# Projecting half of the attention's values inside its first six heads

## The chip, the core and the metric

The kernel runs on one core of a Trainium2 chip. Its time is the device time of one execution in microseconds (us). The core has five engines that each work through their own queue in order: PE (TensorE) multiplies, DVE (VectorE), ACT (ScalarE) and POOL (GpSimd) do the element-wise work, and SP (SyncE) issues transfers. A clock throttle grants PE either its full rate, shown as 1.00, or half of it; a stretch with both shows a value between.

## What is computed

A network of two layers on 512 latent and 256 context tokens of width 1024, in float32. Each layer has a feed-forward part, a mixer and a second feed-forward part. The change touches the mixer of the second layer, a differential attention with 8 heads:

```python
def diff_attention_mixer(h_lat, h_ctx, w_in, w_out, lam_vec, sub_w, lam_init, need_ctx):
    ...
        q, k, v = jnp.split(h @ w_in, (DA_QK, 2 * DA_QK), axis=-1)
    ...
    q_l = apply_axial_rope(q_l, cos, sin).astype(h_lat.dtype)
    k_l = apply_axial_rope(k_l, cos, sin).astype(h_lat.dtype)
    ...
    def diff_attend(q, k, v):
        s = jnp.einsum('bhmqd,bhmkd->bhmqk', q, k).astype(jnp.float32)
        p = jax.nn.softmax(s, axis=-1)
        w = p[:, :, 0] - lam * p[:, :, 1]
        return jnp.einsum('bhqk,bhkv->bhqv', w.astype(v.dtype), v)
```

Queries come from the 512 latent tokens, keys and values from all 768. Each head has two maps of 64 dimensions and 128 value columns; its output is normed and then projected by `w_out`.

## The kernel before

Every projection is made in split precision: an operand is written as a high and a low part, and a product takes three matmuls (`mm3`, lines 157 to 159, with weights as the stationary operand; `mm3t`, lines 1326 to 1328, with tokens as the stationary operand). A weight of 512 KB is loaded to a `raw` buffer (4 of them), cast by ACT (high part) and subtracted by DVE or POOL (low part) into a pair of `r4` buffers (8 buffers, so 4 pairs).

`odd_mixer` first projects all values, `proj_v(0)` and `proj_v(1)`: 144 matmuls of 512 columns each, heads 0 to 3 and heads 4 to 7. The settling of the layer ahead (its second half of tokens) is drawn from inside these passes.

Queries and keys come from a generator, `project_heads`. For each head it makes K (24 matmuls of 256 columns for the context, 24 of 512 for the latent tokens, then rope on DVE and a split) and then Q (24 of 512, rope, split), and gives control back ten times a head. The calls of `next` are placed by numbers: 20 pieces (two heads) are made ahead of the first scores, and then 1, 3, 3, 3 pieces in the four query blocks of a head. So head h carries the projections of head h+2, and heads 6 and 7 carry none.

A query block of 128 rows runs like this: `scores` of the block two ahead (12 matmuls into two double banks), maxima on DVE and exponentials on ACT; `mix_maps` (DVE) joins the two maps; `turn` transposes the result on PE and ACT copies it to the tile `late`; the filler pieces follow; then six matmuls with the values into `po` (line 1297). The norm of the head before (`norm_head`, lines 1254 to 1267) is finished behind block 1. Score and turn tiles share three double banks of PSUM, the filler has one bank (`j`), `po` one. A framework schedules the instructions when the kernel is built: it keeps data dependences and moves instructions of a queue past each other, so a queue's order is not quite the order of the program. `Q` and `K` tiles have two buffers.

Places that the text names by lines of before: L1225 scores, L1228 maxima, L1229 exponentials, L1239 joining of maps, L1246 turn, L1248 copy of the turned block, L1297 value matmuls, L1257 to L1266 norm, L1262 its matmul, L1164 to L1167 rope, L1190 and L1203 copies of projected K and Q, L1212 copy of projected values, L117 and L119 high and low part of a split. In the changed file the lines below 1171 stand 48 to 50 further down (L1225 is L1274 there, L1297 is L1345).

Of the kernel before, what the change touches and what calls it, by code (L numbers as in the profile page):

```python
# [13 lines left out]
F32R = mybir.dt.float32r  # L14
BF16 = mybir.dt.bfloat16
AF = mybir.ActivationFunctionType
# [3 lines left out]
P = 128  # L20
D = 1024
KB = D // P
NCTX = 256
NLAT = 512
NT = NCTX + NLAT
# [17 lines left out]
class Net:  # L43
# [589 lines left out]
    def ffn(self, l, p, halves, nxt, ada=((), ()), table=None, first_of_all=False):  # L633
# [7 lines left out]
        with ExitStack() as st:  # L641
# [67 lines left out]
            cols = (slice(full0, full0 + m), slice(full0 + m, full1))  # L709
            quarter = lambda t, K, N: t[:, K * 4:K * 4 + 4, cols[N]]  # L710
            B = lambda K, N: (quarter(self.xh, K, N), quarter(self.xl, K, N))
            made = {}

            def sums_of_inputs():
# [411 lines left out]
    def odd_mixer(self, nxt):  # L1126
        nc, tc, ins = self.nc, self.tc, self.ins
        W = ins["w_in_odd"]
        H = 8
# [1 line left out]
        mm = nc.tensor.matmul  # L1131


        deep, under, before, fill = 2, 12, 20, (1, 3, 3, 3)
        lam_init = 0.8 - 0.6 * math.exp(-0.3)
        with ExitStack() as st:
            pool = st.enter_context(tc.tile_pool(name="att", bufs=1, reuse_waits="tile"))
# [18 lines left out]
            heads = [{} for _ in range(H)]  # L1156
            swap = [(i + 16) % 32 for i in range(32)]
            n_ = self.tmp
            halfs = (slice(0, 64), slice(64, 128))

            def rope(a):

                b, c = n_("shuf"), n_("rot")
                nc.vector.stream_shuffle(out=b, in_=a, mask=swap)  # L1164
                nc.vector.tensor_mul(out=c, in0=b, in1=cs[:, 1, :])
                nc.vector.tensor_mul(out=b, in0=a, in1=cs[:, 0, :])
                nc.vector.tensor_add(out=a, in0=b, in1=c)  # L1167

            filler = lambda: self.ps("j" if "j" in self.psum_bufs else "h")

            def project_heads():

                for h in range(H):
                    w = self.weights(W[8 + h], "gpsimd")
                    K = pool.tile([P, 2, NT], F32R, tag="K", name="K", bufs=2)
                    a = n_("krot")

                    part = lambda src, c0, c1: self.split(K[:, 0, c0:c1], K[:, 1, c0:c1], src)
                    for i, (c0, c1) in enumerate(((0, NCTX), (NCTX, NT))):
                        ps = filler()[:, :c1 - c0]  # L1180
                        for k in range(KB):
                            ks = slice(k * P, (k + 1) * P)
                            self.mm3(ps, w[0][:, ks], w[1][:, ks], self.xh[:, k, c0:c1], self.xl[:, k, c0:c1],
                                     k == 0, k == KB - 1)
                            if k in ((1, 3, 5) if i else (3,)):
                                yield
                        if i == 0:
                            part(ps, 0, NCTX)
                            yield
                    nc.scalar.copy(out=a, in_=ps)  # L1190
                    rope(a)
                    part(a, NCTX, NT)
                    yield
                    w = self.weights(W[h], "gpsimd")
                    ps = filler()
                    for k in range(KB):
                        ks = slice(k * P, (k + 1) * P)
                        self.mm3(ps, w[0][:, ks], w[1][:, ks], self.xh[:, k, NCTX:], self.xl[:, k, NCTX:],
                                 k == 0, k == KB - 1)
                        if k % 2 and k < KB - 1:  # L1200
                            yield
                    a = n_("qrot")
                    nc.scalar.activation(out=a, in_=ps, func=AF.Copy, scale=0.125)  # L1203
                    rope(a)
                    Q = pool.tile([P, 2, NLAT], F32R, tag="Q", name="Q", bufs=2)
                    self.split(Q[:, 0, :], Q[:, 1, :], a)
                    heads[h].update(q=Q, k=K)
                    yield

            def proj_v(g):  # L1210
                wt = [self.weights(ins["w_v_odd"][g, kk]) for kk in range(4)]
                self.token_major(wt, lambda c, t: nc.scalar.copy(out=v[:, c, g * 512:(g + 1) * 512], in_=t))  # L1212

            def scores(h, qb):

                Q, K = heads[h]["q"], heads[h]["k"]
                qs = slice(qb * P, (qb + 1) * P)
# [49 lines left out]
                nc.sync.dma_start(out=mixd[:, h, NCTX:], in_=y)  # L1267

            v = pool.tile([P, NC, D], F32, name="v")
            proj_v(0)  # L1270
            proj_v(1)
            stream = project_heads()
            for _ in range(under):
                next(stream)  # L1274
# [6 lines left out]
            for h in range(H):  # L1281
                po = self.ps("o")
                dg = pool.tile([P, NLAT], F32, tag="dg", name="dg", bufs=2)
                for qb in range(NLAT // P):
                    e, sm = ready.pop(0)
                    i = 4 * h + qb + deep
                    if i < 4 * H:
                        ready.append(scores(i // 4, i % 4))
                    w = mix_maps(e, sm)
# [3 lines left out]
                    t = turn(w, turned[:, qb % 2])  # L1293
# [83 lines left out]
def layout(inputs):  # L1377
    a = {k: np.asarray(v) for k, v in inputs.items()}
    ca = np.ascontiguousarray
    r = {}  # L1380
    x = np.concatenate([a["ctx"][0], a["x"][0]], axis=0).T
    r["x"] = ca(x.reshape(KB, P, NT).transpose(1, 0, 2))
    r["c"] = ca(np.stack([a["c"][0], a["c_ctx"]]))
    r["ct"] = ca(r["c"].reshape(2, KB, P).transpose(2, 1, 0)).reshape(P, 2 * KB)
    w = a["w_ada"][0, :, :2 * D].reshape(KB // 2, 2, P, 2, 4, 256)
    r["w_ada0"] = ca(w.transpose(4, 0, 2, 1, 3, 5)).reshape(4, KB // 2, P, D)
    r["w_ada"] = ca(a["w_ada"].transpose(0, 2, 1).reshape(DEPTH, N_MOD * KB, P, D))
    r["b_ada"] = ca(a["b_ada"].reshape(DEPTH, N_MOD * KB, P).transpose(2, 0, 1))
    ln = np.stack([a["ln_g"], a["ln_b"]], axis=2)
    r["ln"] = ca(ln.reshape(DEPTH, 3, 2, KB, P).transpose(4, 0, 1, 2, 3))  # L1390

    def units(w):
        lead = w.shape[:-2]
        n = w.shape[-1] // P
        w = w.reshape(lead + (KB, P, n, P))
        m = len(lead)
        return ca(w.transpose(tuple(range(m)) + (m + 2, m + 1, m, m + 3))).reshape(lead + (n, P, D))

    def rows(w):
        lead = w.shape[:-2]  # L1400
        nk = w.shape[-2] // (2 * P)
        nq = w.shape[-1] // 512
        w = w.reshape(lead + (nk, 2, P, nq, 512))
        m = len(lead)
        return ca(w.transpose(tuple(range(m)) + (m + 3, m, m + 2, m + 1, m + 4))).reshape(lead + (nq, nk, P, D))

    r["w_ffn_in"] = units(a["w_ffn_in"])
    r["w_ffn_out"] = rows(a["w_ffn_out"])
    r["w_in_even"] = units(a["w_in_even"][0])
    r["w_v_even"] = rows(a["w_in_even"][0][:, 512:1024])  # L1410
    r["w_out_even"] = rows(a["w_out_even"][0])
    r["hg_lb"] = ca(a["hg_lb"][0].reshape(8, P).T)
    r["hg_norm_w"] = ca(a["hg_norm_w"].reshape(1, P).T)
    r["pool_scale"] = ca(a["pool_scale"][0].reshape(4, P).T)
    r["pool_w"] = ca(a["pool_w"][0].transpose(1, 0, 2))
    r["w_in_odd"] = units(a["w_in_odd"][0])
    r["w_v_odd"] = rows(a["w_in_odd"][0][:, 2048:3072])
    r["w_out_odd"] = rows(a["w_out_odd"][0])
    r["da_lambda"] = ca(a["da_lambda"][0])
    r["da_sub_w"] = ca(a["da_sub_w"].reshape(1, P).T)  # L1420
    pos = np.arange(NLAT)
    inv = (10000.0 ** (-np.arange(0, 32, 2, dtype=np.float32) / np.float32(32))).astype(np.float32)
    ang = np.stack([(pos // 64).astype(np.float32)[None, :] * inv[:, None],
                    (pos % 64).astype(np.float32)[None, :] * inv[:, None]])
    cos, sin = np.cos(ang), np.sin(ang)
    cos = np.concatenate([cos, cos], axis=1).reshape(64, NLAT)
    sin = np.concatenate([-sin, sin], axis=1).reshape(64, NLAT)
    r["rope"] = ca(np.stack([np.tile(cos, (2, 1)), np.tile(sin, (2, 1))], axis=1).astype(np.float32))
    s, t = np.arange(P)[:, None] % 32, np.arange(32)[None, :]
    levels = [s == t] + [(s // (2 * m) == t // (2 * m)) & (s // m != t // m) for m in (1, 2, 4, 8, 16)]  # L1430
    r["msk"] = ca(np.stack(levels, axis=1).astype(np.float32))
    edge = np.ones((4, 16), np.float32)
    for g in range(4):
        w = 2 << g
        for i in range(w // 2):
            edge[g, i] = w / (i + w // 2)
# [23 lines left out]
```

## Time and profile before

| | |
|---|---|
| median of 3 runs | 2761.28 us (2757.34 to 2761.32) |
| the profiled execution | 2760.27 us, span 2758.1 us |
| busy share of the span | PE 97%, DVE 71%, ACT 44%, POOL 32% |
| the attention's value passes to its last norm | some 1992 to 2328 us of the span |

The busy time of PE is not its time at peak: matmuls overlap, each is reported longer than the distance to the next one. Where the text gives the price of a matmul it is the distance between starts. A timeline row gives the start, the duration, the engine, the line and the operands; in brackets stands how long the engine was idle before it and what released it. Rows with a count are several equal instructions, with the time from the first one's start to the last one's end.

### The profile page before, as it was taken

How to read it: one execution, taken by the hardware profiler on the slowest of the kernel's cores; microseconds unless marked ns; L12 is line 12 of the kernel's file. 1: busy time of each engine (PE TensorE's matmuls, PEld its weight loads, DVE VectorE, ACT ScalarE, POOL GpSimd, SP SyncE). 2: the span in 40 equal slices, each digit the busy share in tenths (PEclk: the TensorE clock that was granted, in tenths of full speed). 3: DMA queues.
4: the chain of work that ended last, by engine and by line, in shares of the span. 5: the costliest groups of instructions: out<-in, count | busy, mean ns of one | idle time of the engine just before them, and what ended most of it. 6: DMA issues, size and time to landing. Idle time of an engine off the chain costs nothing. (4 is left out here: it accounts for less than half of the span.)

```text
span 2758.1 us, 43943 instructions
## 1 busy us (share of the span) xinstructions
PE 2667.8 (97%) x17386; PEld 2435.0 (88%) x17386; DVE 1966.3 (71%) x2922; ACT 1221.4 (44%) x1922; POOL 888.1 (32%) x680
## 2 busy tenths in 40 slices
PE   8999999999989999999999999999999998999998
PEld 6999988987778789999888999988887777999997
DVE  4899677847764789977786776556827786787666
ACT  3433433634442533433254444423534655555554
POOL 2545300422110554440055444201422211465302
PEclk9999999999999999999999999999999999999999
DMA  6443266521104334426663432265521112433563
GB/s 250 138 155 129 88 244 231 202 78 68 45 22 168 111 131 143 140 91 221 217 201 117 172 123 78 94 230 197 199 77 47 35 39 79 140 100 116 171 212 129
DMA packets 138770, 374.20 MB, mean 136 GB/s; under 512 B 16066, under 2 KB 47170, under 8 KB 138564
## 3 DMA queue, kind: packets, MB, share of 16 engines
q1 hardware_dynamic: 136256, 369.68, 38.6%
q8 instruction: 136, 2.23, 0.3%
q10 hardware_dynamic: 2308, 1.72, 0.2%
q14 instruction: 70, 0.57, 0.1%
HBM read 337.78 MB, written 33.56 MB: 135 GB/s over the span
## 5 line engine op out<-in xcount | busy, mean ns | idle before, releaser
L117 ACT CAST r4h<-raw 128x1024 fp32r<-128x1024 f32 (+1 forms) x322 | 332.8, 1035 | 625.7 <-PE ps L158 325.0
L157 PE MATMUL ps<-xh,r4h 128*128 128x512 f32 (+2 forms) x1732 | 583.7, 339 | 11.4 <-ACT xh L117 7.6
L158 PE MATMUL ps<-xl,r4h 128*128 128x512 f32 (+2 forms) x1732 | 580.8, 336 | 0.5 <-DVE xl L119 0.4
L159 PE MATMUL ps<-xh,r4l 128*128 128x512 f32 (+2 forms) x1732 | 580.4, 336 | 0.4 <-DVE r4l L119 0.4
L119 DVE TENSOR_TENSOR r4l<-raw,r4h 128x1024 fp32r<-128x1024 f32 (+1 forms) x306 | 373.2, 1221 | 223.5 <-ACT r4h L117 163.6
L157 PEld LDWEIGHTS ps<-xh,r4h 128*128 128x128 f32 x1732 | 326.5, 189 | 41.3 <-ACT xh L117 10.1
L158 PEld LDWEIGHTS ps<-xl,r4h 128*128 128x128 f32 x1732 | 327.4, 189 | 22.9 <-DVE xl L119 2.0
L159 PEld LDWEIGHTS ps<-xh,r4l 128*128 128x128 f32 x1732 | 327.8, 189 | 22.2 <-DVE r4l L119 0.9
L157 PE MATMUL ps<-six,r4h 128*128 128x384 f32 (+1 forms) x852 | 278.3, 327 | 6.0 <-ACT c L788 6.0
L157 PE MATMUL ps<-r4h 128*128 128x512 f32 (+1 forms) x768 | 276.4, 360 | 1.1 <-DVE g L903 1.1
L159 PE MATMUL ps<-r4h,r4l 128*128 128x512 f32 (+1 forms) x768 | 275.3, 359 | 0.7 <-DVE r4l L119 0.7
L158 PE MATMUL ps<-six,r4h 128*128 128x384 f32 (+1 forms) x852 | 275.9, 324 | 0.0
L159 PE MATMUL ps<-six,r4l 128*128 128x384 f32 (+1 forms) x852 | 275.4, 323 | 0.0
L158 PE MATMUL ps<-r4l,r4h 128*128 128x512 f32 (+1 forms) x768 | 275.3, 359 | 0.0
L159 PE MATMUL ps<-r4h,spare 128*128 128x256 f32 (+1 forms) x896 | 262.4, 293 | 9.8 <-DVE spare L119 9.8
L157 PE MATMUL ps<-r4h,spare 128*128 128x256 f32 (+1 forms) x896 | 266.0, 297 | 4.0 <-ACT spare L117 4.0
L158 PE MATMUL ps<-r4l,spare 128*128 128x256 f32 (+1 forms) x896 | 261.4, 292 | 0.0
L760 POOL TENSOR_TENSOR raw<-raw,late 128x512 f32<-128x512 f32 x71 | 93.6, 1319 | 400.4 <-DVE r4l L119 388.5
L119 DVE TENSOR_TENSOR r4l<-late,r4h 128x1024 fp32r<-128x1024 f32 x71 | 106.1, 1495 | 115.1 <-PE ps L158 97.2
L159 PEld LDWEIGHTS ps<-r4h,spare 128*128 128x128 f32 x896 | 174.8, 195 | 13.2 <-DVE spare L119 11.3
L157 PEld LDWEIGHTS ps<-r4h,spare 128*128 128x128 f32 x896 | 175.0, 195 | 8.6 <-ACT spare L117 4.6
L185 DVE SCALAR_TENSOR_TENSOR trash<-spare 128x1024 bf16<-128x1024 f32 x112 | 181.1, 1618 | 1.0 <-DMA spare<-in_w_ada 0.9
(313 smaller groups left out, 5646.6 us busy)
## 6 DMA issues: line engine op xcount, KB each, us to landing
raw<-in_w_ffn_in SPq DMA_DIRECT2D x176, 512.0 KB, 3.5
raw<-in_w_ffn_out SPq DMA_DIRECT2D x176, 512.0 KB, 4.3
spare<-in_w_ada SPq DMA_DIRECT2D x80, 512.0 KB, 5.3
six<-in_w_ada SPq DMA_DIRECT2D x64, 512.0 KB, 5.7
g<-late_g SPq DMA_DIRECT2D x88, 128.0 KB, 2.1
six<-g SPq DMA_DIRECT2D x44, 256.0 KB, 3.7
raw<-in_w_in_even SPq DMA_DIRECT2D x20, 512.0 KB, 3.5
raw<-in_w_in_odd SPq DMA_DIRECT2D x16, 512.0 KB, 3.4
```

The source lines that it names most:

```text
L117: self.copied = self.nc.scalar.copy(out=h, in_=src)
L119: eng.tensor_sub(out=l, in0=src, in1=h.bitcast(F32))
L157: mm(out=ps, lhsT=h, rhs=xh, start=first, stop=False)
L158: mm(out=ps, lhsT=h, rhs=xl, start=False, stop=False)
L159: mm(out=ps, lhsT=l, rhs=xh, start=False, stop=last)
L185: nc.vector.scalar_tensor_tensor(out=self.tmp("trash").bitcast(BF16), in0=r, scalar=1.0, in1=self.c_bc[v], op0=ALU.mult, op1=ALU.mult, acc ...
L760: nc.gpsimd.tensor_sub(out=a12, in0=a12, in1=sums[:, 512:])
```

## The change

The second value pass is taken out of the stretch ahead of the attention. The values of heads 4 to 7 are projected in six pieces inside heads 0 to 5: a piece makes two chunks of 128 tokens for two heads (256 columns), 48 matmuls of 256 columns into one filler bank. Their weights come in another layout, two loads of 512 KB for each two heads; one pair of parts lies in a buffer of its own (`wv`), the other in an `r4` pair that stays taken for three heads, and POOL makes both low parts. The generator is rearranged: ahead of the scores stand K0, Q0 and K1 (16 pieces instead of 20); head h then carries Q of head h+1, a value piece (h < 6) and K of head h+2, in 4, 4, 3 and 3 pieces. Q7 comes in head 6.

```diff
-        deep, under, before, fill = 2, 12, 20, (1, 3, 3, 3)
+        deep, under, before, fill = 2, 12, 16, (4, 4, 3, 3)
...
+            def late_weights(g):
+
+                r = []
+                for i in range(2):
+                    raw = self.raw()
+                    nc.sync.dma_start(out=raw, in_=ins["w_v_late"][g, i])
+                    if i:
+                        r.append(self.pair(raw, 1024, "gpsimd"))
+                    else:
+                        r.append([pool.tile([P, 1024], F32R, tag="wv", name="wv", bufs=2) for _ in range(2)])
+                        self.split(*r[-1], raw, "gpsimd")
+                return r
+
+            def project_values(i):
+
+                g, chunks = i // 3, (i % 3 * 2, i % 3 * 2 + 1)
+                if i == 0:
+                    later.append(late_weights(0))
+                ps = filler()
+                for k in range(KB):
+                    wh, wl = later[g][k // 4]
+                    ws = slice(k % 4 * 256, (k % 4 + 1) * 256)
+                    for x, c in enumerate(chunks):
+                        s = slice(c * P, (c + 1) * P)
+                        self.mm3t(ps[:, x * 256:(x + 1) * 256], wh[:, ws], wl[:, ws], self.xh[:, k, s],
+                                  self.xl[:, k, s], k + x == 0, k + x == KB)
+                    if k % 2 and k < KB - 1:
+                        yield
+                nc.scalar.copy(out=v[:, chunks[0]:chunks[1] + 1, 512 + g * 256:512 + (g + 1) * 256],
+                               in_=ps.rearrange("p (c f) -> p c f", c=2))
+                if i == 2:
+                    later.append(late_weights(1))
+                yield
+
+            def project_heads():
+
+                yield from project_keys(0)
+                yield from project_queries(0)
+                yield from project_keys(1)
+                for h in range(1, H):
+                    yield from project_queries(h)
+                    if h < 7:
+                        yield from project_values(h - 1)
+                    if h + 1 < H:
+                        yield from project_keys(h + 1)
...
-            proj_v(0)
-            proj_v(1)
+            proj_v()
...
-    r["w_v_odd"] = rows(a["w_in_odd"][0][:, 2048:3072])
+    r["w_v_odd"] = rows(a["w_in_odd"][0][:, 2048:2560])
+    w = a["w_in_odd"][0][:, 2560:].reshape(2, 4, P, 2, 256)
+    r["w_v_late"] = ca(w.transpose(3, 0, 2, 1, 4)).reshape(2, 2, P, D)
```

`project_keys` and `project_queries` hold the two halves of the old loop body unchanged.

Where the instructions of a head then stand is read from the orders of the queues. On PE, in a steady head, around the end of K's context part (the matmuls of 256 columns) and the start of its latent part (512 columns), before:

```order
L159 MATMUL ps<-xh,r4l 128x256
L1297 MATMUL ps<-late,v 128x128 x6
L1262 MATMUL pss<-sq,ones_v 128x512
L157 MATMUL ps<-xh,r4h 128x512
L158 MATMUL ps<-xl,r4h 128x512
L159 MATMUL ps<-xh,r4l 128x512
```

and in the changed kernel, where L1345 are the value matmuls, L1274 the scores and L1295 the turn:

```order
L159 MATMUL ps<-xh,r4l 128x256
L1345 MATMUL ps<-late,v 128x128 x5
L157 MATMUL ps<-xh,r4h 128x512
L158 MATMUL ps<-xl,r4h 128x512
L159 MATMUL ps<-xh,r4l 128x512
L157 MATMUL ps<-xh,r4h 128x512
L158 MATMUL ps<-xl,r4h 128x512
L159 MATMUL ps<-xh,r4l 128x512
L1345 MATMUL ps<-late,v 128x128
L1274 MATMUL pss<-K,Q 128x384 x12
L1295 MATMUL pss<-ident,e 128x128 x6
```

Between the two parts of K stood six value matmuls and the norm; now five value matmuls stand there, and the sixth and the next scores come behind two k-steps of the latent part.

On DVE, which reads K's context part out of the filler bank (`K<-ps,K`), in a steady head before, with the norm's steps L357 to L1266:

```order
L119 TENSOR_TENSOR K<-ps,K 128x256
L1239 SCALAR_TENSOR_TENSOR e<-e,sm 128x768
L357 SCALAR_TENSOR_TENSOR t<-sq,t 128x512
L358 TENSOR_SCALAR t<-t 128x512
L359 TENSOR_TENSOR y<-y,t 128x512
L1266 SCALAR_TENSOR_TENSOR y<-o,da_sub_w,y 128x512
L1228 TENSOR_REDUCE sm<-pss 128x1 x2
```

and now, with L1277 the maxima, L1284 to L1288 the joining of the maps and L1315 the norm's last step:

```order
L1277 TENSOR_REDUCE sm<-pss 128x1
L357 SCALAR_TENSOR_TENSOR t<-sq,t 128x512
L1277 TENSOR_REDUCE sm<-pss 128x1
L358 TENSOR_SCALAR t<-t 128x512
L359 TENSOR_TENSOR y<-y,t 128x512
L1284 RECIPROCAL sm<-sm 128x1
L1315 SCALAR_TENSOR_TENSOR y<-o,da_sub_w,y 128x512
L119 TENSOR_TENSOR K<-ps,K 128x256
L1285 SCALAR_TENSOR_TENSOR sm<-sm,nlam 128x1
L1288 SCALAR_TENSOR_TENSOR e<-e,sm 128x768
```

The reading of the context part stood ahead of the norm's steps and now stands behind them.

On ACT, after the last projection, Q7 (its copy is `qrot<-ps`, the high part of its split `Q<-qrot`, the copy of a turned block `late<-pss`), before:

```order
L1203 ACTIVATE qrot<-ps 128x512
L1257 COPY o<-ps 128x512
L1258 ACTIVATE sq<-o 128x512
L117 CAST Q<-qrot 128x512
L1248 COPY late<-pss 128x768
L1229 ACTIVATE e,sm<-pss,sm 128x768 x2
```

and now:

```order
L1204 ACTIVATE qrot<-ps 128x512
L117 CAST Q<-qrot 128x512
L1297 COPY late<-pss 128x768
L1278 ACTIVATE e,sm<-pss,sm 128x768 x2
L1313 COPY sq<-pss 128x512
```

The two steps of the norm between them have gone ahead; the split of Q7 stands ahead of the turned copy in both.

## Rows read from the trace of the kernel before

**Rows 1.** Windows: busy us (and counts) of each engine, granted clock, DMA share, GB/s.

```profile
core 0: us, PE busy (x) PEld busy (x) DVE busy (x) ACT busy (x) POOL busy (x), PEclk, DMA share, GB/s
...
2100.00:2105.00 5.00, 5.00 (x30) 4.26 (x30) 2.00 (x4) 0.80 (x1) 0.00 (x0) 0.66 0.00 0
...
2160.00:2191.50 31.50, 29.80 (x197) 24.38 (x195) 25.39 (x38) 18.73 (x34) 8.46 (x8) 1.00 0.10 34
...
2290.00:2295.00 5.00, 5.00 (x26) 4.34 (x26) 2.08 (x5) 0.99 (x2) 0.45 (x1) 0.50 0.00 0
```

**Rows 2.** Timeline of ACT: the copy of the same value chunk in both passes.

```profile
2025.34 0.59 ACT L1212 COPY v<-ps 128x512 f32<-128x512 f32 x1 [1.29 <-PE ps L1328]
...
2059.07 0.59 ACT L1212 COPY v<-ps 128x512 f32<-128x512 f32 x1 [1.29 <-PE ps L1328]
```

**Rows 3.** Timeline of PE: first matmul of K0's context part and of its latent part.

```profile
2059.58 0.28 PE L157 MATMUL ps<-xh,r4h 128*128 128x256 f32 x1
...
2062.46 0.39 PE L157 MATMUL ps<-xh,r4h 128*128 128x512 f32 x1
```

**Rows 4.** Timeline: first scores, split of K1, first turn, first turn of head 1.

```profile
2082.23 1.14 PE L1225 MATMUL pss<-K,Q 64*128 64x384 f32 x9
...
2087.70 0.62 ACT L117 CAST K<-krot 128x512 fp32r<-128x512 f32 x1 [4.02 <-DVE krot L1167]
...
2099.91 0.85 PE L1246 MATMUL pss<-ident,e 128*128 128x128 f32 x6 [2.09 <-DVE e L1239]
...
2128.34 0.87 PE L1246 MATMUL pss<-ident,e 128*128 128x128 f32 x6
```

**Rows 5.** Timeline of PE: head 3, from its first turn to head 4's.

```profile
2191.46 0.88 PE L1246 MATMUL pss<-ident,e 128*128 128x128 f32 x6
...
2196.46 1.32 PE L1225 MATMUL pss<-K,Q 64*128 64x384 f32 x11 [0.99 <-ACT e L1229]
...
2200.07 1.50 PE L1297 MATMUL ps<-late,v 128*128 128x128 f32 x12
2201.40 1.02 PE L1262 MATMUL pss<-sq,ones_v 128*128 128x512 f32 x2
2203.00 0.51 PE L157 MATMUL ps<-xh,r4h 128*128 128x512 f32 x1 [0.57 <-DVE K L119]
...
2215.41 0.87 PE L1246 MATMUL pss<-ident,e 128*128 128x128 f32 x6
...
2223.00 0.87 PE L1246 MATMUL pss<-ident,e 128*128 128x128 f32 x6
```

**Rows 6.** Timeline of ACT and DVE behind the norm matmul of head 3.

```profile
2202.47 0.58 ACT L1264 COPY sq<-pss 128x512 f32<-128x512 f32 x1
2202.53 0.42 DVE L119 TENSOR_TENSOR K<-ps,K 128x256 fp32r<-128x256 f32 x1
...
2205.07 0.69 DVE L357 SCALAR_TENSOR_TENSOR t<-sq,t 128x512 f32<-128x512 f32 x1 [1.21 <-ACT t L356]
...
2206.99 0.75 DVE L1266 SCALAR_TENSOR_TENSOR y<-o,da_sub_w,y 128x512 f32<-128x512 f32 x1
...
2207.66 1.81 DVE L1228 TENSOR_REDUCE sm<-pss 128x1 f32<-128x768 f32 x2
```

**Rows 7.** Timeline from the end of Q7's matmuls to the last norm.

```profile
2282.59 1.50 PE L1297 MATMUL ps<-late,v 128*128 128x128 f32 x12
...
2287.76 0.62 ACT L117 CAST Q<-qrot 128x512 fp32r<-128x512 f32 x1 [2.39 <-DVE qrot L1167]
...
2289.13 2.93 PE L1297 MATMUL ps<-late,v 128*128 128x128 f32 x12 [3.00 <-ACT late L1248]
...
2305.11 0.87 PE L1246 MATMUL pss<-ident,e 128*128 128x128 f32 x6
...
2309.66 0.87 PE L1246 MATMUL pss<-ident,e 128*128 128x128 f32 x6
...
2326.14 2.07 PE L1262 MATMUL pss<-sq,ones_v 128*128 128x512 f32 x2 [2.73 <-POOL sq L1259]
```

More of the change, by code (lines that the diff above doesn't have):

```diff
@@ L1169, in odd_mixer @@
             filler = lambda: self.ps("j" if "j" in self.psum_bufs else "h")
[L1171 to L1195, printed above, removed]
@@ L1196, in project_heads, with project_keys @@
+            def project_keys(h):
+                w = self.weights(W[8 + h], "gpsimd")
+                K = pool.tile([P, 2, NT], F32R, tag="K", name="K", bufs=2)
+                a = n_("krot")
+                part = lambda src, c0, c1: self.split(K[:, 0, c0:c1], K[:, 1, c0:c1], src)
+                for i, (c0, c1) in enumerate(((0, NCTX), (NCTX, NT))):
+                    ps = filler()[:, :c1 - c0]
                     for k in range(KB):
                         ks = slice(k * P, (k + 1) * P)
-                        self.mm3(ps, w[0][:, ks], w[1][:, ks], self.xh[:, k, NCTX:], self.xl[:, k, NCTX:],
+                        self.mm3(ps, w[0][:, ks], w[1][:, ks], self.xh[:, k, c0:c1], self.xl[:, k, c0:c1],
@@ L1199, in project_heads @@
                                  k == 0, k == KB - 1)
-                        if k % 2 and k < KB - 1:
+                        if k in ((1, 3, 5) if i else (3,)):
                             yield
[L1202 to L1212, printed above, removed]
+                    if i == 0:
+                        part(ps, 0, NCTX)
+                        yield
+                nc.scalar.copy(out=a, in_=ps)
+                rope(a)
+                part(a, NCTX, NT)
+                heads[h].update(k=K)
+                yield
@@ new lines, in project_queries @@
+            def project_queries(h):
+                w = self.weights(W[h], "gpsimd")
+                ps = filler()
+                for k in range(KB):
+                    ks = slice(k * P, (k + 1) * P)
+                    self.mm3(ps, w[0][:, ks], w[1][:, ks], self.xh[:, k, NCTX:], self.xl[:, k, NCTX:],
+                             k == 0, k == KB - 1)
+                    if k % 2 and k < KB - 1:
+                        yield
+                a = n_("qrot")
+                nc.scalar.activation(out=a, in_=ps, func=AF.Copy, scale=0.125)
+                rope(a)
+                Q = pool.tile([P, 2, NLAT], F32R, tag="Q", name="Q", bufs=2)
+                self.split(Q[:, 0, :], Q[:, 1, :], a)
+                heads[h].update(q=Q)
+                yield
@@ new lines, in project_values @@
+            def project_values(i):
+                g, chunks = i // 3, (i % 3 * 2, i % 3 * 2 + 1)
+                if i == 0:
+                    later.append(late_weights(0))
+                ps = filler()
+                for k in range(KB):
+                    wh, wl = later[g][k // 4]
[4 more added lines that the diff above has]
+                                  self.xl[:, k, s], k + x == 0, k + x == KB)
+                    if k % 2 and k < KB - 1:
+                        yield
+                nc.scalar.copy(out=v[:, chunks[0]:chunks[1] + 1, 512 + g * 256:512 + (g + 1) * 256],
+                               in_=ps.rearrange("p (c f) -> p c f", c=2))
+                if i == 2:
+                    later.append(late_weights(1))
+                yield
@@ new lines, in project_heads, with proj_v @@
+            def project_heads():
[8 more added lines that the diff above has]
+                        yield from project_keys(h + 1)
+            later = []
+            def proj_v():
+                wt = [self.weights(ins["w_v_odd"][0, kk]) for kk in range(4)]
+                self.token_major(wt, lambda c, t: nc.scalar.copy(out=v[:, c, :512], in_=t))
```

## The prediction

> **What bounds the kernel now.** I read the page first: PE is busy for nearly all of the span and its clock row is full, so a change pays only where PE idles, waits inside a busy stretch, or runs at half clock. Then the windows of the attention [rows 1]: in head 2 PE is busy 29.80 of 31.50 us, DVE 25.39 and ACT 18.73, so PE is the bound with small holes; and there are two places where the granted clock falls, 0.66 after the attention's first wait and 0.50 after the wait in head 6. Last I read the timeline of PE through the start, one steady head and the last two heads, and looked up what ended each hole. In what follows (h,q) is query block q of head h. "Turn" is the six transposes of a block (L1246), "mix" its six value matmuls (L1297), "scores" its twelve (L1225).
>
> Before the attention starts, PE runs without a hole, so work taken out there comes off the time whole. Inside the heads, work put in costs what PE does, less the holes it fills. The change moves work from the first place to the second; the gain is holes filled, and no arithmetic goes away.
>
> **Unit prices.** The second half of the values is one pass of 144 matmuls of 512 columns. The same copy comes 2025.34 and 2059.07 in the two passes [rows 2]: 33.7 us, or 0.234 a matmul. A matmul of 256 columns costs 0.120: the 24 of K's context part start at 2059.58 and the next piece at 2062.46 [rows 3]. So Q of a head costs 24 x 0.234 = 5.62, K 24 x 0.120 + 5.62 = 8.50, and a value piece 48 x 0.120 = 5.76. The six pieces are 34.6 against 33.7, 0.8 us more work.
>
> **Part 1, the values leave the stretch ahead of the attention: -33.7 us.** K0's first matmul follows the first value pass instead of the second. Its weights are then due 33.7 us earlier; they take the buffers that the second pass's weights had, which showed no wait, so I add nothing.
>
> **Part 2, the start.** From the first scores to the first turn of head 1 it takes 2128.34 - 2082.23 = 46.1 us [rows 4]. Its work before: seven score blocks, four turns, four mixes, Q1, K2, Q2. After: V0 in place of Q2. One block of scores, turn and mix without filler costs 3.37: between the turns at 2215.41 and 2223.00 lie 7.59 us with 18 matmuls of 512 in them [rows 5]. Four blocks 13.5, three more score blocks of 1.25 each 3.75, fillers 5.62 + 5.76 + 8.50 = 19.9: 37.1 us, about the same as before, where 9 us were lost. What is lost after: the first turn needs a chain on DVE of six score maxima (0.9 each, as the pair in [rows 6]), the rope of K1 between them (4.0, as ACT's wait for it in [rows 4]), the low half of K1 (0.7) and the first mix of maps (1.7), 12 to 13 us from the first scores, while PE has 36 score matmuls and 23 of Q1, 9.1 us. So 3.7 are lost there, and I add 1.7 for a slow stretch like 2100 to 2105 (5 us at 0.66) [rows 1]. That gives 42.5, **-3.6 us**. Bounds: no slow stretch and a shorter chain, 41; nothing gained, 46.1.
>
> **Part 3, the steady heads.** The period is 2223.00 - 2191.46 = 31.5 us [rows 5]. Its work is four blocks of 3.37, a norm of 1.0, Q and K 14.1: 28.6. The other 2.9 are holes: scores wait 0.99 for an exponential, because the block ahead has only a 1.5 us piece in front of it; the filler after the norm waits 0.57 until K's context part has been read out of the one filler bank [rows 5]; the rest is pieces split around the wait. After, the pieces are even: Q, then V, then half of K twice. The first hole needs scores to follow too closely on the scores ahead of them; with 4.2 us of filler at least in every block they come 6 us or more later, and it closes. The second stays and moves. The order of PE shows K's 256-column matmuls, then five of the six mix matmuls, then K's next piece, so the cover is 5/6 of a mix, 1.2 us, where it was a mix and a norm. The order of DVE shows the reading of the context part behind the whole norm. By rows [rows 6]: from the copy of the norm at 2202.47 to DVE's first step on it 2.6; a maximum 0.9; its last three steps until 2207.74, 2.0 after that first one; the reading itself 0.42; with gaps some 7.1 us after the norm. PE is there after scores, turn, K's context part and 5/6 of a mix, at 6.0. So a wait of 1.1 us a head. From below: 0.5, the 0.57 of the rows as it is now. From above: 1.7, if the reading takes as long from the end of K's context part as now (2203.00 - 2200.07 = 2.9) with 1.2 of cover. I take 1.1, the sum of the rows in their new order, which lies between them. A head is then 13.5 + 1.0 + 19.9 + 1.1 = 35.5 us.
>
> From the first turn of head 1 to the end of Q7's matmuls it is 2282.59 - 2128.34 = 154.25 us before [rows 4, 7]. After, five heads of 35.5, then the turn (0.63) and Q7 (5.62 and a step) that now stand in head 6: 183.8. **+29.5 us.** DVE's 25.4 us spread over 35.5 instead of 31.5, and ACT takes on 0.6 for a piece and 0.7 for weights a head. Neither comes near the period. The weights' low halves go to POOL, which is busy 8.5 us a head, and the four new loads of 512 KB stand in the SP queue two uses ahead.
>
> **Part 4, the tail.** From Q7's end to the last norm: 2326.14 - 2282.59 = 43.55 us [rows 7]. Here Q7's rope was on DVE, and ACT waited 2.39 for it in the cast that stands ahead of the copy of the turned weights; PE waited 3.00 for that copy and then ran at 0.50. After, the same two instructions stand in the same order behind Q7, one block later: I expect the stall and the slow stretch to stay and only move to (6,1). What goes is one bare block, since Q7 now fills (6,0): 2309.66 - 2305.11 = 4.55 [rows 7]. 39.0, **-4.5 us**. If the stall falls short of the clock's drop the tail gains 2.5 more; if norm and stall add up in one block it loses 2.
>
> **Sum.** -33.7 - 3.6 + 29.5 - 4.5 = -12.3 us. The profiled execution took 2760.27 us (span 2758.1 and 2.2 around it), 1.0 under the median of the runs. 2760.3 - 12.3 = **2748.0 us**.
>
> **The clock, weighed.** The granted clock was 0.66 in the stretch after a wait of 2.09 us [rows 1, 4] and 0.50, its lower level of 1.2 GHz, after one of 3.00 [rows 1, 7]. In a head built like the one with waits of 0.99 and 0.57 [rows 5] it was 1.00. The Trainium skill (TensorE: Matmul & The Clock Gate, "A second HAM failure mode: psum-queue depth-cycling") says that small idle times between matmul groups which cycle through PSUM can make the clock go back and forth between its levels. By that rule the new wait on the one filler bank would cost clock in every head, the second rival below; the steady heads of this trace do not agree so far.
>
> **Rivals.** (1) The holes stay and only change place: PE meets in each head as much waiting as now (2.9 instead of 1.1), for example because DVE's order, with the norm ahead of the reading, runs later than its rows sum to. 5 x 1.8 = 9.0 back: 2757.0; with the start's 3.6 also back 2760.6. For it: the stated cover is smaller than before, and every wait here is set by in-order queues of ACT and DVE. Against: the 0.99 has a cause that the even pieces remove. (2) Slower: the wait on the filler bank reaches 2.0 us and halves the clock behind it, six times. Each costs 1.0 us more wait and 1.7 (5 us at 0.66) to 2.5 (5 us at 0.50) of slow matmuls: 6 x 2.7 to 6 x 3.5, 16 to 21 us, 2764 to 2769. It decides from a wait of 2.0 us, twice my estimate; against it stands that the longest wait of head 3 is 0.99 [rows 5] and that head 2, built alike, ran at 1.00 [rows 1]. (3) That the pieces don't come where they are said to be is ruled out by the order of PE: the 48 value matmuls stand in block 1 of heads 0 to 5, Q of the next head in block 0.
>
> **How the numbers follow.** My forecast 0.79, rival 1 0.15, rival 2 0.06. The bounds: heads 0.5 to 1.7 of wait, -3 to +3; start -1.5 to +3.6; tail -2.5 to +2. All the low ends together give 2741.0, all the high ends 2756.6; rival 1 at 2757.0 takes the upper end to 2758. Range 2741 to 2758. A measurement of this kernel tells some 0.2%, 5.5 us, from no change. Faster by more than that (under 2755.8), the forecast: 0.79; within, rival 1: 0.15; slower, rival 2: 0.06.
>
> **What would show it.** In the profile after: the first scores some 33.7 us earlier; no wait of scores for exponentials in heads 1 to 5; one wait a head of PE for DVE's K, about 1.1 us; a period between first turns of 35.5 us; a wait of 2.5 to 3 us for the turned copy in (6,1) with the clock at half behind it; and the last norm starting 12 us earlier than at 2326.14. I am wrong if the period is above 37 us, or if the granted clock is under 1.00 within heads 1 to 5, and in the first step if K0 waits for its weights.

## The result, and the profile after

The changed kernel takes 2744.09 us (median, 2742.66 to 2746.52) beside 2759.31 of the kernel before: a ratio of 0.9946, 95% interval 0.9929 to 0.9964. Two later sets of runs gave 2739.56 beside 2759.32 and 2741.75 beside 2760.11. By these medians the change takes off 15 to 20 us; 12.3 were forecast.

The profiled execution has a span of 2742.4 us. I cut the attention of every trace at the same five events: the first copy of values on ACT, the first scores, the first turn of head 1, the first turn of head 6, the last norm. The first and the last of these are 310.20 us apart before and 291.36 after. Ahead of the first copy both kernels run the same instructions, and yet the three profiles of the changed kernel reach it at 2018.99, 2018.18 and 2015.64 (before at 2015.94). That is scatter between executions, so in what follows I compare the stretch from the first copy to the last norm and not spans.

Timeline of ACT, PE and DVE of the changed kernel: first value copy, the scores of head 0 and the wait between them, DVE's first joining of maps, first turn of head 0, the scores of a later block, first turn of head 1 (these answer to [rows 2, 4]):

```profile
2018.99 2.02 ACT L1261 COPY v<-ps 128x512 f32<-128x512 f32 x4
...
2051.55 2.35 PE L1274 MATMUL pss<-K,Q 64*128 64x384 f32 x18
...
2055.69 1.33 PE L1274 MATMUL pss<-K,Q 64*128 64x384 f32 x6 [0.43 <-ACT e L1278]
...
2057.61 1.34 PE L1274 MATMUL pss<-K,Q 64*128 64x384 f32 x6
...
2059.53 1.31 PE L1274 MATMUL pss<-K,Q 64*128 64x384 f32 x6
...
2062.21 1.94 DVE L1288 SCALAR_TENSOR_TENSOR e<-e,sm 128x768 f32<-128x768 f32 x2
...
2064.14 0.82 PE L1295 MATMUL pss<-ident,e 128*128 128x128 f32 x6
...
2076.24 1.34 PE L1274 MATMUL pss<-K,Q 64*128 64x384 f32 x12
...
2093.23 0.87 PE L1295 MATMUL pss<-ident,e 128*128 128x128 f32 x6
```

One value pass stands ahead of the scores now: 2051.55 - 2018.99 = 32.56 us, where it was 66.29. The wait of 2.09 before the first turn [rows 4] is gone.

Timeline of PE of the changed kernel, head 3 (answers to [rows 5]; the trace holds two records for each value matmul, so a mix of six is x12):

```profile
2163.43 0.88 PE L1295 MATMUL pss<-ident,e 128*128 128x128 f32 x6
...
2180.14 1.02 PE L1311 MATMUL pss<-sq,ones_v 128*128 128x512 f32 x2
...
2185.95 1.28 PE L1345 MATMUL ps<-late,v 128*128 128x128 f32 x10
...
2187.74 0.51 PE L157 MATMUL ps<-xh,r4h 128*128 128x512 f32 x1 [0.51 <-DVE K L119]
...
2198.40 0.87 PE L1295 MATMUL pss<-ident,e 128*128 128x128 f32 x6
```

The period is 2198.40 - 2163.43 = 34.97 us. The wait of scores for an exponential (0.99) is gone; one wait is left, for DVE's reading of K's context part.

Timeline of PE and, between its rows, of ACT, from the end of Q7's matmuls to the last norm (answers to [rows 7]):

```profile
2274.65 1.50 PE L1345 MATMUL ps<-late,v 128*128 128x128 f32 x12
...
2279.36 0.62 ACT L117 CAST Q<-qrot 128x512 fp32r<-128x512 f32 x1 [3.63 <-DVE qrot L1167]
2279.89 0.79 ACT L1297 COPY late<-pss 128x768 f32<-128x768 f32 x1
...
2280.73 1.60 PE L1345 MATMUL ps<-late,v 128*128 128x128 f32 x12 [2.53 <-ACT late L1297]
...
2291.09 1.60 PE L1345 MATMUL ps<-late,v 128*128 128x128 f32 x12 [0.89 <-ACT late L1297]
...
2310.35 2.07 PE L1311 MATMUL pss<-sq,ones_v 128*128 128x512 f32 x2 [2.74 <-POOL sq L1308]
```

The stall for the turned copy stands where it was forecast, in (6,1). ACT's queue still holds the cast of Q7 ahead of that copy. The 0.89 is what a block of the tail without filler waits for the copy anyway.

Windows (columns as in [rows 1]), first head 3 and the stretch around the stall in the changed kernel, then the same five us around the same stall in its third profile:

```profile
2163.43:2198.40 34.97, 34.46 (x245) 29.95 (x243) 25.32 (x38) 19.30 (x35) 8.34 (x8) 1.00 0.09 31
...
2280.00:2285.00 5.00, 4.27 (x32) 3.27 (x32) 3.52 (x7) 4.27 (x8) 0.45 (x1) 1.00 0.01 2
```

```profile
2277.00:2282.00 5.00, 4.59 (x20) 3.26 (x22) 2.75 (x5) 2.67 (x6) 0.45 (x1) 0.66 0.00 0
```

In the heads the granted clock is 1.00. Behind the stall of 2.53 us it stayed at 1.00 in one execution and was 0.66 in the others.

### The profile page after: what moved, and what is told of

Its sections match the earlier page's. It is cut to its first block, busy times and chain, and to the rows that moved or that the text cites. A ratio compares the mean times of both kernels' runs of the same rounds, so it can differ in the third digit from the quotient of the medians.

```text
span 2742.4 us, 44233 instructions
## 1 busy us (share of the span) xinstructions
PE 2660.8 (97%) x17530; PEld 2437.4 (89%) x17530; DVE 1962.8 (72%) x2918; ACT 1220.4 (45%) x1922; POOL 900.3 (33%) x684
```

## The experiments

Every ratio is against runs of the kernel before on the same chip in the same set. This table has the four stretches of every profile (us). Clock is the granted clock of five us from the stall of head 6 on ((6,0) before and in e2_values, (6,1) in the others):

| | values | start | heads 1 to 5 | end | sum | clock | ratio, 95% |
|---|---|---|---|---|---|---|---|
| before | 66.29 | 46.11 | 156.92 | 40.88 | 310.20 | 0.50 | 1 |
| changed | 32.56 | 41.68 | 175.10 | 42.02 | 291.36 | 1.00 | 0.9946 [0.9929, 0.9964] |
| after_again | 32.56 | 41.74 | 175.11 | 43.68 | 293.09 | 0.66 | 0.9931 [0.9919, 0.9943] |
| changed_third | 32.56 | 41.71 | 175.10 | 43.69 | 293.06 | 0.66 | 0.9933 [0.9921, 0.9945] |
| e1_queries | 66.29 | 36.46 | 155.49 | 43.68 | 301.92 | 0.66 | 0.9971 [0.9961, 0.9981] |
| e2_values | 32.56 | 47.29 | 177.10 | 41.20 | 298.15 | 0.50 | 0.9954 [0.9942, 0.9967] |
| e3_uneven | 32.55 | 43.74 | 192.04 | 43.68 | 312.01 | 0.66 | 1.0007 [0.9997, 1.0018] |
| e4_q7_dve | 32.54 | 41.74 | 175.10 | 41.16 | 290.54 | 1.00 | 0.9925 [0.9914, 0.9937] |
| e5_norm2 | 32.56 | 41.74 | 171.04 | 44.22 | 289.56 | 0.66 | 0.9929 [0.9917, 0.9941] |
| e6_start | 30.72 | 45.10 | 175.08 | 42.03 | 292.93 | 1.00 | 0.9941 [0.9929, 0.9952] |
| e7_all | 30.72 | 45.09 | 171.05 | 42.16 | 289.02 | 1.00 | 0.9922 [0.9910, 0.9934] |
| e8_two | 32.56 | 41.72 | 171.05 | 42.15 | 287.48 | 1.00 | 0.9904 [0.9888, 0.9919] |

The stretches of the changed kernel repeat within 0.1 us over its three profiles, except the end, which has two values 1.7 us apart, one for each clock. So a single profile can tell apart edits that the times of some runs can't. The kernel before and each edit have one profile; the slow clock in it is that of one execution.

**The changed kernel again (after_again, changed_third).**

> The changed kernel once more, so that the others are compared on the same chip. Both theories: 12 to 19 us under the kernel before; period of a steady head 35.0 us, a wait of 0.5 us a head for K's context part.

> The changed kernel once more, unaltered, so that the version below stands beside it in the same hour: a ratio of 0.993 to 0.995 against the kernel before.

Measured: 2739.56 and 2741.75 us, 19.8 and 18.4 us under the kernel before in the same set. The start, the heads and the value pass repeat to 0.1 us.

**One part alone: the queries (e1_queries) or the values (e2_values).**

```diff
--- e1_queries: values as before, queries half a head later
+        deep, under, before, fill = 2, 12, 16, (4, 0, 3, 3)
...
-                    if h < 7:
-                        yield from project_values(h - 1)
...
+            proj_v(0)
+            proj_v(1)
--- e2_values: values in the heads, queries a head ahead as before
+        deep, under, before, fill = 2, 12, 20, (5, 3, 3, 3)
...
+                for h in range(H):
+                    if h > 1:
+                        yield from project_values(h - 2)
+                    yield from project_keys(h)
...
```

> Values as before, only the queries half a head later: Q1 is projected inside head 0, Q7 in head 6, blocks carry 4, 0, 3, 3 pieces. Theory H (the gain is holes of PE that are filled, from either half of the change): no work is removed, yet 10 to 14 us under the kernel before: about -9 at the start (46.1 to about 37 us from the first scores to head 1's first turn), +3 to +5 in heads 1 to 5 with Q7, -4.5 to -8 in the tail. Rival V (the value pieces alone bring the gain, the query shift only makes room): within 2 us of the kernel before.

> Queries as before (a head ahead), only the values of heads 4 to 7 go into blocks 0 of heads 0 to 5 ahead of K's first half. Theory H: 8 to 16 us under the kernel before: first scores 33.7 us earlier, the 0.99 us wait of scores for exponentials gone from heads 1 to 5, so a steady head of about 35.2 us, and the stall of about 3 us with a slow clock still in head 6. Rival Q (the query shift alone brings the gain, moving values costs its 0.8 us): 0 to 2 us over the kernel before. If both halves fill the same holes, the two single gains add up to clearly more than the whole.

Measured: 2751.15 us and 2746.27 us, 8.2 and 13.1 under the kernel before. The values lie in their range; the queries miss theirs of 10 to 14. Their start came as expected (-9.65), but from head 1's first turn on they take 1.4 us more, where between 5.0 less and 0.5 more was expected. In the stretch the queries alone take off 8.3 us, the values 12.1, together 20.3, and the whole change 17.1 to 18.8. To see where they overlap, subtract from each stretch the matmul time that the edit only moves into or out of it (Q 5.62; a value piece 5.76, one in the start and five in heads 1 to 5). What is left is time that PE saved:

| | start | heads 1 to 5 | end |
|---|---|---|---|
| e1_queries | -9.65 + 5.62 = -4.0 | -1.4 | 2.80 - 5.62 = -2.8 |
| e2_values | 1.18 - 5.76 = -4.6 | 20.18 - 28.8 = -8.6 | +0.3 |
| changed | -4.43 - 5.76 + 5.62 = -4.6 | 18.18 - 28.8 = -10.6 | 1.14 - 5.62 = -4.5 |

Not all of it is holes. Windows of the kernel before behind its stall and over its heads 1 to 5, and of heads 1 to 5 of the changed kernel:

```profile
2288.00:2296.00 8.00, 6.49 (x30) 5.55 (x30) 5.08 (x8) 3.31 (x7) 0.45 (x1) 0.57 0.00 1
...
2128.34:2285.26 156.92, 148.73 (x972) 121.96 (x970) 126.97 (x190) 92.83 (x166) 32.90 (x32) 1.00 0.10 36
```

```profile
2093.23:2268.33 175.10, 172.25 (x1212) 149.74 (x1211) 128.97 (x188) 98.23 (x174) 43.97 (x36) 1.00 0.13 45
```

Slow clock took 3.4 us of the end before (8 us at 0.57) and 1.7 of its start (5 us at 0.66 [rows 1]). In the end, e2_values has the same 3.4, e1_queries 1.7 and the changed profile none; without it the end's row is -1.1, +0.3 and -1.1, so the end belongs to the queries. In the heads PE's idle time fell from 8.2 to 2.9 us, which is half of the 10.6; the other half is no idle time in these windows, and where it lies was not shown.

The heads add up (1.4 + 8.6 = 10.0 of 10.6). The start's saving is the same one for both parts: with either of them the wait of 2.09 us and the slow clock behind it are gone. That counts some 4.0 us twice. Less the 0.6 in the heads and 0.3 in the end by which the whole is better than the sum, it makes the 3.2 us by which the single gains exceed the whole in the two profiles with e1_queries' clock (1.5 in the one whose clock stayed up).

Timeline of PE, the queries alone, one head's waits:

```profile
2163.49 0.44 PE L1272 MATMUL pss<-K,Q 64*128 64x384 f32 x1 [0.67 <-ACT Q L117]
2164.45 1.31 PE L1272 MATMUL pss<-K,Q 64*128 64x384 f32 x11 [0.52 <-ACT e L1276]
...
2170.82 0.50 PE L157 MATMUL ps<-xh,r4h 128*128 128x512 f32 x1 [0.30 <-DVE K L119]
```

Without a value piece in block 1, the holes stay in the heads and change place (0.67 + 0.52 + 0.30). So it is the filler in every block that closes them, as the prediction said of the 0.99. The values alone, with filler in every block, show no wait above 0.25 us in four of heads 1 to 5, and 0.74 in head 2.

**The pieces made uneven again (e3_uneven).**

```diff
-        deep, under, before, fill = 2, 12, 16, (4, 4, 3, 3)
+        deep, under, before, fill = 2, 12, 16, (0, 8, 3, 3)
...
-                    for _ in range(fill[qb]):
+                    for _ in range((4, 4, 3, 3)[qb] if h == 6 else fill[qb]):
```

> The changed kernel with the same pieces, but none in block 0 and eight (Q and the value piece) in block 1 of heads 0 to 5; head 6 as in the changed kernel. Theory H: the wait of scores for exponentials comes back because two blocks of scores follow each other with about 1 us of filler between: 1.0 to 2.0 us a head, a period of 36 to 37 us, 6 to 12 us over the changed kernel. Rival (the hole hung on the order of Q and K, not on how much filler a block has): within 2 us of the changed kernel.

Measured: 2759.71 us; the whole gain is gone, although the same work stands in the same heads (only Q and the value piece share a block, and block 0 has next to none). Timeline of PE, head 1 and then head 2 of this kernel, and the windows of head 1, of the place behind the second wait, and of head 3:

```profile
2096.20 1.31 PE L1274 MATMUL pss<-K,Q 64*128 64x384 f32 x11 [1.30 <-ACT e L1278]
...
2158.96 0.51 PE L157 MATMUL ps<-xh,r4h 128*128 128x512 f32 x1 [2.28 <-DVE K L119]
```

```profile
2091.15:2129.53 38.38, 36.93 (x245) 31.40 (x243) 25.42 (x38) 19.41 (x35) 8.31 (x8) 0.96 0.10 35
...
2158.00:2163.00 5.00, 4.04 (x16) 2.94 (x16) 0.90 (x2) 0.00 (x0) 0.00 (x0) 0.66 0.01 3
...
2170.72:2207.44 36.72, 35.32 (x245) 30.05 (x243) 25.36 (x38) 19.46 (x35) 8.25 (x8) 1.00 0.09 30
```

Each of heads 1 to 5 has a wait of 1.24 to 1.30 us of scores for an exponential, as expected. Head 3, with the clock up, has a period of 36.72 instead of 34.97. Behind two of these waits, in heads 1 and 4, the granted clock fell (0.96 over head 1, 0.66 in the five us from 2097); behind the other three it did not. In head 2 it fell behind another wait, 2.28 us for DVE's reading of K's context part: that is the second rival of the prediction as it was put, a wait on the filler bank of more than 2.0 us. Heads 1 and 4 take 38.3 us and more, head 2 41.2. The loss of 20 us against the changed kernel is more than the 6 to 12 expected; the three slow stretches are some 5 of it (1.7 each).

**The stall in (6,1) (e4_q7_dve).**

```diff
-                self.split(Q[:, 0, :], Q[:, 1, :], a)
+                if h == H - 1:
+                    nc.vector.tensor_copy(out=Q[:, 0, :], in_=a)
+                    nc.vector.tensor_sub(out=Q[:, 1, :], in0=a, in1=Q[:, 0, :].bitcast(F32))
+                else:
+                    self.split(Q[:, 0, :], Q[:, 1, :], a)
```

> The changed kernel with one edit: the high part of the last head's queries is cast by DVE, and not by ACT. Theory (ACT does its queue in order, and the turned copy that the mix of block (6,1) wants stands behind the cast of the queries, which waits for PE's last query matmul): the wait of 2.53 us ahead of the mix in head 6 shrinks to under 1 us, the granted clock stays at 1.00 there, and the time lies 1.5 to 2.5 us below the changed kernel's, up to 4 us where the clock had fallen behind the wait; against the kernel before a ratio near 0.9925. Rival (the copy is late for another reason, as DVE's reading of the queries' sum): the wait stays within 0.5 us of 2.53 and the time is the changed kernel's, a ratio of 0.993 to 0.9945.

Measured: 2739.31 us. Timeline of this kernel, ACT's turned copy and PE's waits in head 6:

```profile
2275.59 0.80 ACT L1301 COPY late<-pss 128x768 f32<-128x768 f32 x1 [2.50 <-PE pss L1299]
```

```profile
2276.44 1.60 PE L1349 MATMUL ps<-late,v 128*128 128x128 f32 x12 [0.89 <-ACT late L1301]
...
2279.82 1.33 PE L1278 MATMUL pss<-K,Q 64*128 64x384 f32 x11 [0.56 <-ACT e L1282]
...
2282.98 1.27 PE L1349 MATMUL ps<-late,v 128*128 128x128 f32 x9 [1.02 <-ACT late L1301]
```

ACT now waits for PE's turn and not for Q7, and PE's stall falls from 2.53 to the 0.89 of a block without filler. So the cause was ACT's in-order queue. The gain was smaller than the 1.5 to 4 us expected: the stretch is 0.8 us shorter than in the changed profile whose clock stayed up, 2.5 shorter than in the two whose clock fell, since of the 1.64 us 0.56 came back in the next scores. The time alone doesn't separate it from the changed kernel.

**The wait in each head (e5_norm2).**

```diff
-                    if qb == 1:
+                    if qb == 2:
```

> The changed kernel with one edit: the norm of a head is finished behind block 2 of the next head, and not behind block 1, so that DVE comes to the context part of the keys before the steps of the norm. Theory (the wait of 0.52 us in each head is DVE's, which has the norm's steps ahead of the keys in its queue): that wait goes in the five heads that show it, the heads' period falls from 34.97 to about 34.45 us, the work of PE alone, and the time by 2.5 to 3 us. Rival (DVE's total work or another reader of the same bank sets the period): the wait moves to another row of the head, the period stays at 34.9 to 35.0, and the time is the changed kernel's within 0.5 us.

Measured: 2739.53 us. Timeline of PE and DVE of this kernel in head 4, where DVE reads K, then windows of its head 5 and of the stretch behind the stall, and a window of head 3 of e2_values:

```profile
2215.69 1.50 PE L1345 MATMUL ps<-late,v 128*128 128x128 f32 x12
...
2217.07 0.42 DVE L119 TENSOR_TENSOR K<-ps,K 128x256 fp32r<-128x256 f32 x1
...
2217.55 0.74 PE L157 MATMUL ps<-xh,r4h 128*128 128x512 f32 x1
```

```profile
2228.26:2262.47 34.21, 34.21 (x244) 29.88 (x243) 26.37 (x40) 19.95 (x36) 4.29 (x6) 1.00 0.14 47
...
2275.00:2280.00 5.00, 5.00 (x30) 4.13 (x30) 3.00 (x5) 1.70 (x4) 0.45 (x1) 0.66 0.00 0
```

```profile
2166.72:2201.82 35.10, 35.01 (x245) 29.97 (x243) 25.77 (x38) 19.24 (x35) 8.80 (x8) 1.00 0.09 31
```

The wait is gone and PE is busy for the whole period, which falls by 0.76 us to 34.21. That is 0.25 more than the 0.51 in brackets. Whether a wait costs more than its own length is not shown: the edit also moves the norm's matmuls, and a head of e2_values is busy for 35.01 of 35.10 us, so the same work takes 0.8 us more or less in another order, without a wait in either. Over heads 1 to 5 the edit gains 4.1 us. Some comes back in the end: with the clock up it is 42.15 in e8_two, with this edit, and 41.16 in e4_q7_dve, without it. In this execution the clock fell behind the unchanged stall of 2.53, and the end took 44.22; the stretch is 3.5 us shorter than in the two profiles of the changed kernel whose clock fell too. The time alone does not separate the two kernels.

**The start (e6_start), and all three edits (e7_all).**

```diff
-        deep, under, before, fill = 2, 12, 16, (4, 4, 3, 3)
+        deep, under, before, fill = 2, 10, 14, (4, 4, 3, 3)
...
-                yield from project_keys(1)
                 for h in range(1, H):
                     yield from project_queries(h)
+                    if h == 1:
+                        yield from project_keys(1)
...
-                    for _ in range(fill[qb]):
+                    for _ in range(6 if h + qb == 0 else fill[qb]):
```

> The changed kernel with the start in another order: keys 0, queries 0 and queries 1 ahead of the first head's turned maps, and keys 1 as the filler of its blocks, where the changed kernel has keys 1 ahead and queries 1 as filler. Theory (in the start PE is short of work that needs no map: keys are 8.5 us of matmuls and queries 5.6, so the longer one covers more of the first maps' chain on ACT and DVE): from the first scores to head 1's first turn 38 to 40 us instead of 41.7, the later heads unchanged at 35.0, the time 2 to 3.5 us below the changed kernel's. Rival (the chain of the first maps is covered already, and keys 1 come late for the scores of head 1): a new wait of 1 us or more ahead of head 1's scores, and the time is the changed kernel's or up to 2 us above it.

> The three edits together: the last queries cast by DVE, the norm behind block 2, keys 1 as the filler of head 0. If the three waits are separate holes of PE on one chain, their gains add up: 6 to 8 us below the changed kernel, a ratio of 0.990 to 0.991 against the kernel before. If they share a cause (DVE's queue, which gets more work in head 6 by the first edit and later norms by the second), less than 4 us below it, a ratio of 0.992 or more, with a wait of PE for DVE in head 6 or 7 that the changed kernel does not show.

Measured: 2743.92 us and 2738.93 us. Timeline of PE, start of e6_start:

```profile
2048.34 2.73 PE L1275 MATMUL pss<-K,Q 64*128 64x384 f32 x18 [0.97 <-ACT Q L117]
...
2059.63 0.50 PE L157 MATMUL ps<-xh,r4h 128*128 128x512 f32 x1 [0.92 <-DVE K L119]
```

My theory of the start fell. The scores come 1.84 us earlier (keys 1 out, queries 1 in, less the new wait of 0.97 for the split of Q0), but the start is 3.4 longer: 1.6 us lost. Work that needs no map was not what was lacking: PE's waits in the changed kernel's start are 0.43 and 0.28 us. With keys 1 as filler PE meets two waits for ACT's and DVE's splits that queries 1 in that place avoid. With all three edits the ratio is 0.9922, where 0.990 to 0.991 was expected of separate waits. By this number a shared cause would be right, but its sign, a wait for DVE in head 6 or 7, is not there; the stretch of 289.02 has the norm's 4.1 us gained and 1.6 lost in the start.

**The two edits that gained (e8_two):** those of e4_q7_dve and e5_norm2.

> The changed kernel with the two edits whose traces showed a gain, and the start as it is: the last queries cast by DVE and the norm behind block 2. Theory (the two waits are separate, and the start with keys 1 as filler cost 1.6 us in each kernel that had it): from the first copy of the values to the last norm 287.5 us, 3.9 less than the changed kernel's 291.4, a ratio of 0.9915 to 0.992 and below the kernel with all three edits. Rival (the two edits share DVE in heads 6 and 7, so that what the norm's place gives in the heads comes back in the tail): 289.5 us or more, and the time within 2 us of the changed kernel's.

Measured: 2732.98 us (2732.70 to 2735.12), a ratio of 0.9904 (0.9888 to 0.9919), beside 2741.75 and 0.9933 of the changed kernel in the same set. The stretch is 287.48 us, as expected; the ratio is below the 0.9915 to 0.992 expected. Of the 8.8 us between the two medians the stretch holds 5.6, and 1.7 of these are the clock. Windows of its head 5 and of the place where the stall was, and its last norm:

```profile
2226.34:2260.56 34.22, 34.22 (x245) 29.88 (x243) 26.37 (x40) 19.96 (x36) 4.30 (x6) 1.00 0.14 47
2271.00:2276.00 5.00, 4.34 (x30) 3.18 (x30) 4.47 (x8) 2.24 (x5) 1.00 (x1) 1.00 0.00 0
```

```profile
2302.71 1.12 PE L1315 MATMUL pss<-sq,ones_v 128*128 128x512 f32 x2 [2.73 <-POOL sq L1312]
```

The two waits were separate: the stretch is 3.9 us shorter than in the changed profile whose clock stayed up, the norm's 4.1 and the cast's 0.8 less the 1.0 that the later norm gives back in the end. This version beats both kernels.

## Why the prediction was right, step by step

The time lies in the forecast's range, and in the heads and the tail what happened is the forecast's own mechanism: even pieces close holes of PE, and a stall moves. But the measured saving in the stretch is 17.1 to 18.8 us and not 12.3; each term but the first was too cautious, and the start came out near its number for another reason.

**Part 1, values out: -33.7 forecast, 32.56 - 66.29 = -33.73 measured.** The weights of K0 were not late.

**Part 2, the start: -3.6 forecast, -4.4 measured.** The first turn comes 2064.14 - 2051.55 = 12.6 us after the first scores, within the forecast 12 to 13, but not for the reason given, and that is luck. The forecast let PE do 9.1 us of work and wait 3.7 for DVE. In the trace PE waits 0.43 in this stretch. DVE begins its first joining of maps at 2062.21 and takes 1.0 for it, so that PE, which reaches the turn at 2064.14, is the later one. PE's own work was longer than its price. The forecast had 36 score matmuls at the 1.25 us for twelve of a steady block; here three groups of six came by themselves, and six took as long as twelve do later (1.31 to 1.34 us in the rows of the first timeline, beside 1.34 for the twelve at 2076.24). By an estimate from these rows, 0.6 us more for each of the three groups, that is some 2 of the 3 us that were missing in the price. The slow stretch of 1.7 us that I added did not come, since the wait of 2.09 ahead of it is gone; the granted clock of the start is 1.00. From the first turn to head 1's first turn it took 29.1 where my sum has 28.0; that 1.1 I can't place.

**Part 3, the heads: +29.5 forecast, +27.2 measured** (2274.65 - 2093.23 = 181.42, less 154.25). The work without the wait was right: 34.97 - 0.51 = 34.46, forecast 34.4. The mis-sized term is the wait, 1.1 forecast and 0.51 to 0.78 measured, at the low bound. Timeline of ACT and DVE behind the norm of head 3 in the changed kernel (answers to [rows 6]):

```profile
2181.20 0.59 ACT L1313 COPY sq<-pss 128x512 f32<-128x512 f32 x1 [1.61 <-PE pss L1311]
...
2183.81 0.69 DVE L357 SCALAR_TENSOR_TENSOR t<-sq,t 128x512 f32<-128x512 f32 x1 [0.31 <-ACT t L356]
2184.42 0.95 DVE L1277 TENSOR_REDUCE sm<-pss 128x1 f32<-128x768 f32 x1
2185.29 0.42 DVE L358 TENSOR_SCALAR t<-t 128x512 f32<-128x512 f32 x1
2185.74 0.82 DVE L359 TENSOR_TENSOR y<-y,t 128x512 f32<-128x512 f32 x1
2186.49 0.15 DVE L1284 RECIPROCAL sm<-sm 128x1 f32<-128x1 f32 x1
2186.60 0.75 DVE L1315 SCALAR_TENSOR_TENSOR y<-o,da_sub_w,y 128x512 f32<-128x512 f32 x1
2187.27 0.42 DVE L119 TENSOR_TENSOR K<-ps,K 128x256 fp32r<-128x256 f32 x1
```

PE came to the place when I said: its mix ends at 2187.23, 6.0 us after the copy of the norm at 2181.20. DVE was done at 2187.69, 6.5 after it and not 7.1. The first step came after 2.6 as read. Behind it my durations come to 6.6 in all with that 2.6, and the rest of the 7.1 were gaps for which no row stood. There was next to none (0.03 us at most between the steps above): on DVE the next step starts before the last one's time is over (0.95 of a maximum takes 0.87 from start to start, 0.69 takes 0.61). Where one engine runs steps back to back, the distance between starts is the price, on DVE as I had it on PE.

**Part 4, the tail: -4.5 forecast; measured 35.70 - 43.55 = -7.9 in one execution and -6.2 in two (37.4 us).** The stall and its place were right. In the two with the slow clock the stall is 2.53 and not 3.00 (0.5), and the slow stretch behind it costs 1.7 us and not the 3.4 of the kernel before; that is 0.6 more than the 1.6 by which they beat the forecast, and this 0.6 stays unplaced. In the one with the clock up there are 1.7 more: the case that I had priced at 2.5, from five us at 0.50.

**The first rival** (the holes only change place) is what the queries alone do in the heads, and the values close. **The second** came true in e3_uneven alone, in head 2, with a wait of 2.28 on the filler bank. In two other heads of that execution waits of 1.30 and 1.24 us, of scores for an exponential, were enough, so the distance to it was smaller than I argued: the changed kernel's 0.5 to 0.8 against 1.24, not against 2.0. The Trainium skill (TensorE: Matmul & The Clock Gate, "A second HAM failure mode: psum-queue depth-cycling") says that small idle times between groups of matmuls can make the clock swing. The runs agree for waits of 1.24 us and more, and not always; the queries alone had three waits in each of four heads (about 0.67, 0.52, 0.30) and stayed at 1.00.

## What to carry to other kernels

Moving work from a stretch without holes into one with holes pays by the holes it fills, and here it filled them only when every block got some: the same work in uneven pieces gave back the whole gain, some 5 of the 20 us by the clock. Before adding up the gains of two edits, ask whether they fill the same hole. When a wait names an in-order engine, look for what stands ahead in that engine's queue: moving one cast to another queue and one norm a block later took another 4 to 6 us off the stretch here, 1.7 of them only where the clock had fallen.

## What was not expected of the hardware

The same wait of 2.53 to 2.54 us for the same instruction was followed by a full clock in two profiles (changed, e6_start) and by 0.66 in five (after_again, changed_third, e1_queries, e3_uneven, e5_norm2), 1.7 us apart. Waits of 1.24 to 1.30 us were followed by a lower clock in two of five heads of one execution. So whether the clock falls behind a wait of this size was not settled by its length here. What decides it stays open; no run was made for it.

Six score matmuls by themselves took as long as twelve that stood together (1.33 and 1.34 us). A price read from a steady block therefore did not hold in the start, where the scores came in smaller groups.
